# Longest products first in the scores, a shared reciprocal, an earlier column sum for the down factors, and two norms paced later

## The chip, the cores and the metric

The kernel runs on one core of one Trainium2 chip. The metric is the device time of one execution in microseconds (us); the time before is 2511.2 us, the median of three runs (2506.69 to 2511.34 us). Lower is better.

## What is computed

Two layers of a transformer over 1024 latent and 256 context tokens, width 1024, in float32. Cut to what matters here:

```python
for i in range(DEPTH):                                        # 2 layers
    h = modulate(rmsnorm(x, norm_pre_mix[i]), sh1, sc1)       # hc for the context tokens
    p = h @ w_in[i]                                           # queries, keys, values, Fourier channels
    attn = windowed_gqa_with_context(q, k, v, kc, vc, sink[i])
    four = fourier_mix(u, w_fourier[i])
    mix = concatenate([attn, four]) @ w_out[i]
    x_mid = x + g1 * rmsnorm(mix, norm_post_mix[i])
    hf = modulate(rmsnorm(x_mid, norm_pre_ffn[i]), sh2, sc2)
    x = x_mid + g2 * rmsnorm(swiglu(hf, w_gate[i], w_up[i], w_down[i]), norm_post_ffn[i])
# swiglu(h, g, u, d) = (silu(h @ g) * (h @ u)) @ d, hidden width 2816
# attention: 8 query heads, 2 key/value heads, head size 64; a query sees latent keys at
# distance <= 128, all 256 context keys and one sink logit per head, under one softmax
```

## The kernel before, in words

All activations stay in SBUF with channels on partitions (`X`: 128 x 8 x 1280). The tokens are worked on in two blocks, A and B: 640 tokens each in the first layer, 512 each in the second, where the context needs no output. Precision is built from pairs: each operand is split into a high and a low part, and a product is three matmuls (high x high, low x high, high x low). `gemm` (L518) does that for the input and output projections, `ffn_up` (L1084) for gate and up with seven half-size products in place of eight, `ffn_down` (L1215) for down, with its weights scaled and split on the way in (L1207 on ScalarE, L1208 on VectorE).

**Order.** The program is written as Python generators that `mix` interleaves: it always steps the one that is least far along for the cost that it was given, so `(side, 27)` means that the norm work beside a product is paced as if it had 27 steps. A bare `yield` in a generator is a step with nothing in it. The order in which the program emits instructions is their priority; the framework's scheduler (`schedule_with_timeline_sim=True`) then fixes the order on each engine's queue before the run, and `high_priority(offset=n)` moves what is inside it n places ahead. On the chip each queue runs in that order.

**Attention.** `Pair` handles two heads of one block of 128 queries. `score` (L191 to L216) fills a PSUM tile of two banks: the sink logit in one column (L197, a one-column product of a table of ones), the window of up to 384 latent keys (L201 high, L206 low, on the same bank), the two masks added as 128-column bf16 products with the identity (L203, L205), and 256 context keys (L207, L208). Then VectorE takes the negated row maximum (L215) and ScalarE the exponential with its sum `su` (L216). `turn` transposes the probabilities on TensorE (L226) and splits them (L230, L231). `value` multiplies by the values (L244); at its first step it makes a reciprocal tile of 128 columns out of the two sums of the two heads (L238), which `finish` transposes (L252) and multiplies in (L259). The attention runs beside the Fourier mixing and the projections of block B; there are 144 scores (16 of them for context queries, with no window) and 72 pairs.

**Norms.** `stats` squares and adds the eight tiles of a block, sums over partitions with one-column products (L667, tile `nps`) and computes the inverse root of the mean (L673 to L679, at high priority). `spread` (L689, tile `rps`) transposes that back over the tokens into a PSUM tile of the same pool (`sc`, two buffers) as the scores and the products of the projections, and copies it (L691). `postnorm` is `stats`, then `spread`, then eight steps: load the residual (SyncE's queue), scale (L712), add (L782 on VectorE or GpSimd), and store. `scaled` and `prenorm` do the norm ahead of a product.

**Layer turn.** Between the layers, the second block's `postnorm` runs beside the first three tiles of the next input projection (6, 7, 8); then the second block's `xstats` and `scaled` (the variable `side`) run beside tiles 1, 0, 2, 3, 4, 5 of it.

**Down factors.** After `ffn_up` each of the 11 chunks of the hidden layer has an exponent `he` per partition. `down_scale(blk)` makes of them and of the norms of the down weights a factor per chunk (`dn`) and one power of two for all partitions (`dback`). For the maximum over partitions it uses `highest` (L602 to L605): a product with the identity that lays the column out as a row, a VectorE maximum, and a product that spreads it back. `down_scale(0)` comes after the whole of `ffn_up`, `down_scale(1)` after the down product of block 0. Then `hidden` loads the spilled hidden chunks back from DRAM on SyncE's queue (L1189), and `ffn_down` loads the down weights on the same queue (L1202).

The steps of `ffn_up` are interleaved too: while the matrix `m` of `seq` takes its steps 1 to 5, the last two steps of the matrix before it are put between them. The last four matrices are (block 0, chunk 10, gate), (0, 10, up), (1, 10, gate), (1, 10, up).

Of the kernel before, what the change touches and what calls it, by code (L numbers as in the profile page):

```python
# [174 lines left out]
class Pair:  # L175
# [15 lines left out]
    def score(self, h):  # L191

        net, nc, w, g, n = self.net, self.nc, self.w, self.g, self.n
        s = net.sc.tile([P, 1024], F32, tag="sc", name="score")
        q = self.qs[:, 2 * self.u + h, :]
        hd = 4 * g + 2 * self.u + h
        nc.tensor.matmul(s[:, 511 - w:512 - w], net.bf1[:], net.sink[:, self.l, hd:hd + 1], start=True, stop=True)  # L197
        if w:
            loc = s[:, 512 - w:512]
            ls = slice(C + P * self.k0, C + P * self.k1)  # L200
            nc.tensor.matmul(loc, q, net.KHI[g][:, ls], start=True, stop=False)  # L201
            if n > 0:
                nc.tensor.matmul(loc[:, 0:P], net.bf[:, 0:P], net.bf[:, P:2 * P], start=False, stop=False)  # L203
            if n < NB - 1:
                nc.tensor.matmul(loc[:, w - P:w], net.bf[:, 0:P], net.bf[:, 2 * P:3 * P], start=False, stop=False)  # L205
            nc.tensor.matmul(loc, q, net.KLO[g][:, ls], start=False, stop=True)  # L206
        nc.tensor.matmul(s[:, 512:512 + C], q, net.KHI[g][:, 0:C], start=True, stop=False)  # L207
        nc.tensor.matmul(s[:, 512:512 + C], q, net.KLO[g][:, 0:C], start=False, stop=True)  # L208
        sv = s[:, 511 - w:512 + C]
        hs = slice(h, h + 1)  # L210
        p = net.PP[net.npp % len(net.PP)][:, 0:w + C + 1]
        net.npp += 1
        self.pp.append(p[:, 1:])
        with net.tc.high_priority(offset=AHEAD_OF):
            nc.vector.tensor_reduce(self.ng[:, hs], sv, axis=AX.X, op=ALU.max, negate=True)  # L215
            nc.scalar.activation(p, sv, AF.Exp, bias=self.ng[:, hs], accum_out=self.su[:, hs])  # L216
# [17 lines left out]
    def value(self, j):  # L234
        net, nc = self.net, self.nc
        if j == 0:
            self.out = net.qsp.tile([P, 2, P], F32, tag="pvl", name="pvl")
            nc.vector.reciprocal(self.out[:, 0].rearrange("p (h d) -> p h d", h=2), self.su[:].unsqueeze(2).broadcast_to([P, 2, HD]))  # L238
            self.pv = net.ps.tile([P, 384], F32, tag="ps", name="pv")
# [23 lines left out]
class Net:  # L263
# [504 lines left out]
    def postnorm(self, l, which, a, b, done=None, share=False, y=None):  # L768
# [5 lines left out]
        y = y or x  # L774
        yield from self.stats(y, w, "post")
        r = self.spread("post", w)
        for k in range(KD):
# [268 lines left out]
    def ffn_up(self, l, blocks, seq):  # L1046
# [92 lines left out]
        for m, after in zip(seq + [None], seq[1:] + [None, None]):  # L1139
# [4 lines left out]
            for n, who in enumerate((now, now, before, now, before, now, now)):  # L1144
                if who is not None and next(who, 0) is None:
                    yield c
                if n == 4 and after:
                    ready(after)
            before = now

# [13 lines left out]
    def down_scale(self, blk):  # L1164


        nc, r = self.nc, self.dn[blk]
        one = float(1 << 23)
        nc.vector.tensor_scalar(r[:].bitcast(I32), self.he[:, blk], one, -14 * one, op0=ALU.mult, op1=ALU.add)
        m = self.sm.tile([P, 2], F32, tag="fm", name="dm")  # L1170
        nc.vector.tensor_reduce(m[:, 0:1], r[:], axis=AX.X, op=ALU.max)
        nc.vector.scalar_tensor_tensor(m[:, 1:2], m[:, 0:1], m[:, 0:1], self.dmax[:], op0=ALU.mult, op1=ALU.mult)
        nc.vector.tensor_scalar(m[:, 1:2], m[:, 1:2], 1e-30, None, op0=ALU.max)
        self.power(self.dback[blk], self.highest(m[:, 1:2]).bitcast(I32), 24, 204)
        nc.vector.tensor_scalar(r[:], r[:], self.dback[blk][:, 0].bitcast(F32), None, op0=ALU.mult)

# [52 lines left out]
    def program(self):  # L1229
# [26 lines left out]
        for l in range(L):  # L1256
# [5 lines left out]
            else:  # L1262
                mix((self.inproj(l, 0, (6, 7, 8)), cost(3, KD, BW - C)), (first, 8))
                self.rope_tables()
# [3 lines left out]
            else:  # L1268
                mix((self.inproj(l, 0, (1, 0, 2, 3, 4, 5)), cost(6, KD, BW - C)), (side, 14))
            blocks = [A, B] if l == 0 else [(C, C + 512), (C + 512, T)]  # L1270
# [17 lines left out]
            def done(k, a, b, last=last):  # L1288
                if last:
                    nc.sync.dma_start(self.io["out"][:, k, a - C:b - C], self.X[:, k, a:b])  # L1290
                else:
# [4 lines left out]
                         self.prenorm(l, *blocks[0], "A", self.G[0]))  # L1296
            mix((self.outproj(l, *blocks[1]), cost(KD, KD, w)), (side, 27))
            self.G[1] = operands(l % 2)
# [7 lines left out]
            up = self.ffn_up(l, blocks, seq)  # L1306
            mix((part(up, 14 * AHEAD - 2), 2 * AHEAD * one), (side, 45))
            mix((part(up, 14 * AHEAD - 7), 2 * AHEAD * one), (self.down_norms(l), 24))
            mix((up, one * (44 - 4 * AHEAD)), (mod(0, 1), 64), (iter(()) if last else self.norms(l + 1), 2 * AHEAD))
            self.down_scale(0)  # L1310
            places = self.hidden(l, blocks)
# [4 lines left out]
            if not last:  # L1316
# [3 lines left out]
                side = chain(norm, self.xstats(*A, "A"), self.scaled(l + 1, 0, *A, "A"))  # L1320
                mix(down(1, 0, w, lambda m: self.X[:, m, a1:b1]), (side, 30), (pre, 8 * AHEAD))
                self.new_arena((l + 1) % 2)
# [41 lines left out]
```

## Time and profile before

| | before |
|---|---|
| runs | 2511.2, 2506.69, 2511.34 us |
| profiled execution: time | 2504.05 us |
| profiled execution: first to last instruction (span) | 2502.2 us |
| mean granted TensorE clock | 0.980 |
| TensorE matmul busy (PE) | 2352.4 us, 17224 instructions |
| VectorE busy (DVE) | 1787.2 us, 3462 instructions |
| ScalarE busy (ACT) | 1344.7 us, 2587 instructions |
| GpSimd busy (POOL) | 196.6 us, 204 instructions |
| DMA | 406.83 MB, mean 163 GB/s |

How to read it: the profile is of one execution, so a duration in it is set against 2504.05 us and not against the median. "Busy" for TensorE counts a matmul from its start to its modelled end, and matmuls overlap; the distance from one start to the next tells what one costs. "PEld" is the load of the stationary operand. A row of the timeline has the start and the length in us, the engine, the source line, the operation, what it writes and reads, and in brackets how long the engine stood idle before it and what ended that. A row of the windows has the busy time of each engine in a stretch, then the granted clock, the share of the DMA engines that was busy, and GB/s.

### The profile page before, as it was taken

To read this page: it belongs to the slowest core of one execution; us is meant where nothing else is said; L and a number is where in the kernel's file an instruction comes from. 1 tells how busy PE (TensorE), PEld (TensorE's weight loads), DVE (VectorE), ACT (ScalarE), POOL (GpSimd) and SP (SyncE) were. 2 spreads that over 40 slices of the span, in tenths; PEclk is the share of its full clock that TensorE was granted. 3 is DMA by queue.
4 is the path that set the end of the run, shared out by engine and by line. 5 is a ranking of instruction groups with operands and counts; after the bars stand their busy time and mean duration, and the time that the engine had idled before them with its cause. 6 is when DMAs were issued, how large, how long until landed. Compare 5 with 4: busy or idle time off the path is not lost. (4 is left out here: it accounts for less than half of the span.)

```text
span 2502.2 us, 44066 instructions
## 1 busy us (share of the span) xinstructions
PE 2352.4 (94%) x17224; PEld 1900.2 (76%) x17224; DVE 1787.2 (71%) x3462; ACT 1344.7 (54%) x2587; POOL 196.6 (8%) x204
## 2 busy tenths in 40 slices
PE   7998988999999999999999989989999999989997
PEld 5887877897776666666767779988778888874586
DVE  5588787767837887778774588797777577765485
ACT  4575556657525445434544345566674456545473
POOL 0222210010000000000000033210100000000000
PEclk9999989999999999999999989999999999999998
DMA  8535423568554344459873231101596422246474
GB/s 309 206 102 167 160 98 107 184 236 284 203 185 148 108 129 165 156 192 373 269 246 129 91 123 47 35 18 51 186 338 222 161 72 69 77 142 208 132 254 125
DMA packets 157377, 406.83 MB, mean 163 GB/s; under 512 B 17488, under 2 KB 34288, under 8 KB 157168
## 3 DMA queue, kind: packets, MB, share of 16 engines
q1 hardware_dynamic: 147952, 389.33, 46.2%
q10 hardware_dynamic: 9216, 14.68, 1.6%
q8 instruction: 135, 2.21, 0.4%
q14 instruction: 74, 0.61, 0.1%
HBM read 339.19 MB, written 64.76 MB: 161 GB/s over the span
## 5 line engine op out<-in xcount | busy, mean ns | idle before, releaser
L1084 PE MATMUL p<-ffn,ww 128*128 128x320 f16 (+1 forms) x7392 | 921.9, 287 | 25.5 <-ACT ww L464 5.5
L1084 PEld LDWEIGHTS <-ww 128*128 128x128 f16 x7392 | 722.7, 98 | 220.8 <-issue 23.5
L1215 PEld LDWEIGHTS <-wd 128*128 128x128 f16 x3696 | 363.6, 99 | 164.0 <-ACT wd L1207 5.8
L1215 PE MATMUL acc<-hid,wd 128*128 128x320 f16 (+2 forms) x2544 | 335.4, 294 | 3.5 <-ACT wd L1207 3.2
L1208 DVE SCALAR_TENSOR_TENSOR wd<-raw,dn,wd 128x256 f16<-128x256 f32 x440 | 186.4, 480 | 132.6 <-ACT wd L1207 132.0
L1207 ACT ACTIVATE wd<-raw,dn 128x256 f16<-128x256 f32 x440 | 187.2, 496 | 146.0 <-PE acc L1215 87.2
L518 PE MATMUL accn<-arena,hi 128*128 128x320 f32 (+1 forms) x992 | 252.2, 327 | 5.6 <-DVE X L259 2.0
L518 PE MATMUL acc<-arena,hi 128*128 128x320 f32 (+2 forms) x928 | 209.0, 330 | 5.6 <-ACT X L1038 3.8
L1215 PE MATMUL acc<-X,wd 128*128 128x320 f16 (+1 forms) x1152 | 195.0, 331 | 0.9 <-ACT wd L1207 0.9
L518 PEld LDWEIGHTS accn<-arena,hi 128*128 128x128 f32 x992 | 173.2, 190 | 16.3 <-DVE arena L231 2.7
L518 PEld LDWEIGHTS acc<-arena,hi 128*128 128x128 f32 x928 | 154.8, 190 | 23.4 <-ACT X L1038 5.3
L518 PE MATMUL accn<-arena,lo 128*128 128x320 f32 (+1 forms) x496 | 159.8, 325 | 1.7 <-DVE lo L400 1.7
L674 POOL TENSOR_TENSOR nr<-nm,mhalf 128x5 f32<-128x5 f32 (+2 forms) x17 | 18.2, 1069 | 1708.0 <-DVE nm L673 1708.0
L465 DVE SCALAR_TENSOR_TENSOR ww<-raw,sp,ww 128x1024 f16<-128x1024 f32 x112 | 125.4, 1147 | 27.3 <-ACT ww L464 27.1
L464 ACT ACTIVATE ww<-raw,sp 128x1024 f16<-128x1024 f32 x112 | 109.9, 1033 | 59.4 <-DVE raw L479 51.0
L400 DVE TENSOR_TENSOR lo<-raw,hi 128x1024 fp32r<-128x1024 f32 x77 | 101.6, 1320 | 55.0 <-ACT hi L399 39.9
L230 ACT CAST arena<-tp 128x512 fp32r<-128x512 f32 (+1 forms) x184 | 96.6, 528 | 76.6 <-PE tp L226 74.2
L216 ACT ACTIVATE A<-score,ng 128x641 f32<-128x641 f32 (+2 forms) x144 | 106.6, 741 | 46.9 <-PE tp L226 30.1
L215 DVE TENSOR_REDUCE ng<-score 128x1 f32<-128x641 f32 (+2 forms) x144 | 106.3, 740 | 28.6 <-PE score L208 27.3
L518 PE MATMUL acc<-arena,lo 128*128 128x320 f32 (+2 forms) x464 | 125.0, 327 | 0.1
L399 ACT CAST hi<-raw 128x1024 fp32r<-128x1024 f32 x77 | 80.6, 1047 | 75.1 <-PE acc L518 28.7
L448 ACT ACTIVATE junk<-raw 128x1024 bf16<-128x1024 f32 x88 | 92.3, 1051 | 42.1 <-DMA raw<-in_wup 19.2
(231 smaller groups left out, 3724.4 us busy)
## 6 DMA issues: line engine op xcount, KB each, us to landing
raw<-in_wdown SPq DMA_DIRECT2D x112, 512.0 KB, 4.6
ww<-wc SPq DMA_DIRECT2D x96, 512.0 KB, 4.3
raw<-in_wgate SPq DMA_DIRECT2D x60, 512.0 KB, 4.6
raw<-in_wup SPq DMA_DIRECT2D x60, 512.0 KB, 4.4
wm<-in_wada SPq DMA_DIRECT2D x96, 256.0 KB, 4.3
raw<-in_wdown SPq DMA_DIRECT2D x56, 384.0 KB, 4.2
raw<-in_win SPq DMA_DIRECT2D x40, 512.0 KB, 3.6
wada<-in_wada SPq DMA_DIRECT2D x39, 512.0 KB, 4.4
```

The costliest lines, as they stand in the source:

```text
L215: nc.vector.tensor_reduce(self.ng[:, hs], sv, axis=AX.X, op=ALU.max, negate=True)
L216: nc.scalar.activation(p, sv, AF.Exp, bias=self.ng[:, hs], accum_out=self.su[:, hs])
L230: nc.scalar.copy(ph, tp[:, 0:256 * n])
L400: nc.vector.tensor_tensor(lo[:, 0:w], raw[:, 0:w], hi[:, 0:w].bitcast(F32), op=ALU.subtract)
L448: self.nc.scalar.activation(junk[:], raw[j][:], AF.Square, accum_out=self.ss[:, j, i:i + 1])
L464: nc.scalar.activation(hi, src, AF.Copy, scale=s)
L465: nc.vector.scalar_tensor_tensor(lo, src, s, hi, op0=ALU.mult, op1=ALU.subtract)
L518: self.nc.tensor.matmul(ps, wt[:, ks], xt[:, a:b], start=(k == 0 and i == 0), stop=(k == n - 1 and i == 2))
L1084: nc.tensor.matmul(ps, w[:, at:at + P], G[:, k, x, c, 0:h], start=(start and k + t == 0), stop=(k == KD // 2 - 1 and t == 2), skip_group_c ...
L1207: nc.scalar.activation(wt[:, 0, c], raw[:, c], AF.Copy, scale=r)
L1208: nc.vector.scalar_tensor_tensor(wt[:, 1, c], raw[:, c], r, wt[:, 0, c], op0=ALU.mult, op1=ALU.subtract)
L1215: nc.tensor.matmul(out, wt[:, e, k], xs[x][:, s, u:v], start=(f + s + i == 0), stop=(f == NP - 1 and s == 1 and i == 2))
```

## The change

- `score`: the order of its products on TensorE. Before: sink, high window, masks, low window, context. After: high window, low window, context high and low, then the masks, then the sink.
- `value`: the reciprocal is taken of the two columns in place, and a copy spreads it over the 128 columns.
- `postnorm`: two empty steps between `stats` and `spread`. The costs given to `mix` for the norms go up where they hold a postnorm (8 to 9, 27 to 29, 45 to 46, 30 to 32). For the second block's norm ahead of the next layer's input projection the cost goes from 14 to 10, so its steps come later relative to the product.
- `down_scale`: in place of the maximum over partitions a sum over partitions, as one product of a bf16 table of ones with a 16-bit column; all at high priority. `down_scale(0)` is emitted within `ffn_up`, after the second step of the last matrix.

```diff
@@ score
-        nc.tensor.matmul(s[:, 511 - w:512 - w], net.bf1[:], net.sink[:, self.l, hd:hd + 1], start=True, stop=True)
         if w:
             loc = s[:, 512 - w:512]
             ls = slice(C + P * self.k0, C + P * self.k1)
             nc.tensor.matmul(loc, q, net.KHI[g][:, ls], start=True, stop=False)
-            if n > 0:
-                nc.tensor.matmul(loc[:, 0:P], net.bf[:, 0:P], net.bf[:, P:2 * P], start=False, stop=False)
-            if n < NB - 1:
-                nc.tensor.matmul(loc[:, w - P:w], net.bf[:, 0:P], net.bf[:, 2 * P:3 * P], start=False, stop=False)
-            nc.tensor.matmul(loc, q, net.KLO[g][:, ls], start=False, stop=True)
+            nc.tensor.matmul(loc, q, net.KLO[g][:, ls], start=False, stop=False)
         nc.tensor.matmul(s[:, 512:512 + C], q, net.KHI[g][:, 0:C], start=True, stop=False)
         nc.tensor.matmul(s[:, 512:512 + C], q, net.KLO[g][:, 0:C], start=False, stop=True)
+        if w:
+            if n > 0:
+                nc.tensor.matmul(loc[:, 0:P], net.bf[:, 0:P], net.bf[:, P:2 * P], start=False, stop=(n == NB - 1))
+            if n < NB - 1:
+                nc.tensor.matmul(loc[:, w - P:w], net.bf[:, 0:P], net.bf[:, 2 * P:3 * P], start=False, stop=True)
+        nc.tensor.matmul(s[:, 511 - w:512 - w], net.bf1[:], net.sink[:, self.l, hd:hd + 1], start=True, stop=True)
@@ value
-            nc.vector.reciprocal(self.out[:, 0].rearrange("p (h d) -> p h d", h=2), self.su[:].unsqueeze(2).broadcast_to([P, 2, HD]))
+            nc.vector.reciprocal(self.su[:], self.su[:])
+            nc.vector.tensor_copy(self.out[:, 0].rearrange("p (h d) -> p h d", h=2), self.su[:].unsqueeze(2).broadcast_to([P, 2, HD]))
@@ postnorm
         yield from self.stats(y, w, "post")
+        yield
+        yield
         r = self.spread("post", w)
@@ ffn_up
                 if n == 4 and after:
                     ready(after)
+                if n == 1 and m == (1, NP - 1, 1):
+                    self.down_scale(0)
@@ down_scale
-        nc.vector.tensor_scalar(m[:, 1:2], m[:, 1:2], 1e-30, None, op0=ALU.max)
-        self.power(self.dback[blk], self.highest(m[:, 1:2]).bitcast(I32), 24, 204)
+        with self.tc.high_priority(offset=1000):
...
+            nc.vector.tensor_scalar(sq[:], m[:, 1:2], 1e-30, None, op0=ALU.max)
+            ps = self.ps.tile([P, 8], F32, tag="ps", name="dsum")[:, 0:1]
+            nc.tensor.matmul(ps, self.bf1[:], sq[:], start=True, stop=True)
+            self.power(self.dback[blk], ps.bitcast(I32), 24, 204)
@@ program
-                mix((self.inproj(l, 0, (6, 7, 8)), cost(3, KD, BW - C)), (first, 8))
+                mix((self.inproj(l, 0, (6, 7, 8)), cost(3, KD, BW - C)), (first, 9))
-                mix((self.inproj(l, 0, (1, 0, 2, 3, 4, 5)), cost(6, KD, BW - C)), (side, 14))
+                mix((self.inproj(l, 0, (1, 0, 2, 3, 4, 5)), cost(6, KD, BW - C)), (side, 10))
-            mix((self.outproj(l, *blocks[1]), cost(KD, KD, w)), (side, 27))
+            mix((self.outproj(l, *blocks[1]), cost(KD, KD, w)), (side, 29))
-            mix((part(up, 14 * AHEAD - 2), 2 * AHEAD * one), (side, 45))
+            mix((part(up, 14 * AHEAD - 2), 2 * AHEAD * one), (side, 46))
-            self.down_scale(0)
-                mix(down(1, 0, w, lambda m: self.X[:, m, a1:b1]), (side, 30), (pre, 8 * AHEAD))
+                mix(down(1, 0, w, lambda m: self.X[:, m, a1:b1]), (side, 32), (pre, 8 * AHEAD))
```

More of the change, by code (lines that the diff above doesn't have):

```diff
@@ L1168, in down_scale @@
         one = float(1 << 23)
[L1169 to L1173, printed above, removed]
-        self.power(self.dback[blk], self.highest(m[:, 1:2]).bitcast(I32), 24, 204)
-        nc.vector.tensor_scalar(r[:], r[:], self.dback[blk][:, 0].bitcast(F32), None, op0=ALU.mult)
+        with self.tc.high_priority(offset=1000):
+            nc.vector.tensor_scalar(r[:].bitcast(I32), self.he[:, blk], one, -14 * one, op0=ALU.mult, op1=ALU.add)
+            m = self.sm.tile([P, 2], F32, tag="fm", name="dm")
+            sq = self.sm.tile([P, 1], BF16, tag="sq", name="dq")
+            nc.vector.tensor_reduce(m[:, 0:1], r[:], axis=AX.X, op=ALU.max)
+            nc.vector.scalar_tensor_tensor(m[:, 1:2], m[:, 0:1], m[:, 0:1], self.dmax[:], op0=ALU.mult, op1=ALU.mult)
+            nc.vector.tensor_scalar(sq[:], m[:, 1:2], 1e-30, None, op0=ALU.max)
+            ps = self.ps.tile([P, 8], F32, tag="ps", name="dsum")[:, 0:1]
+            nc.tensor.matmul(ps, self.bf1[:], sq[:], start=True, stop=True)
+            self.power(self.dback[blk], ps.bitcast(I32), 24, 204)
+            nc.vector.tensor_scalar(r[:], r[:], self.dback[blk][:, 0].bitcast(F32), None, op0=ALU.mult)
     def hidden(self, l, blocks):
```

## The prediction

> **What bounds the kernel now.** I read the page first, then TensorE's busy time in the two stretches of attention, then TensorE's own waits, and then a timeline at each place that the edits touch.
>
> ```profile
> PE 2352.4 (94%) x17224; PEld 1900.2 (76%) x17224; DVE 1787.2 (71%) x3462; ACT 1344.7 (54%) x2587; POOL 196.6 (8%) x204
> ```
> ```profile
> 99.00:500.00 401.00, 361.18 (x2519) 319.14 (x2518) 314.90 (x565) 252.85 (x538) 61.79 (x72) 0.97 0.44 145
> 1509.00:1766.00 257.00, 246.11 (x1756) 225.19 (x1755) 203.73 (x386) 156.69 (x359) 50.77 (x60) 0.99 0.12 37
> ```
> ```profile
> PE score L197 <- ACT A L216: 15.1, 15, 2.3
> PE rps L689 <- DVE nr L679: 14.4, 7, 6.5
> PE fps L605 <- DVE hm L1121: 6.5, 2, 3.5
> ```
>
> TensorE is busy 94% of the span, so only two things shorten the run: cheaper matmul sequences, and TensorE's waits. The first two columns of the windows are the length of the stretch and TensorE's busy time: it idles 401.0 - 361.2 = 39.8 us in attention of layer 1 and 10.9 us in layer 2. VectorE (fourth number) is at 79% in both. Three of the largest rows of TensorE's waits are places that the change touches: the score buffer, the transposes of a norm, the factors of down.
>
> **Scores.** One two-mask score, and full-clock products of 384 columns behind each other:
>
> ```profile
> 254.27 0.17 PE L197 MATMUL score<-sink,bf 128*128 128x1 bf16 x1
> 254.30 0.42 PE L201 MATMUL score<-arena,qs 128*128 128x384 f32 x1
> 254.56 0.23 PE L203 MATMUL score<-bf 128*128 128x128 bf16 x1
> 254.62 0.22 PE L205 MATMUL score<-bf 128*128 128x128 bf16 x1
> 254.65 0.42 PE L206 MATMUL score<-arena,qs 128*128 128x384 f32 x1
> 254.91 0.28 PE L207 MATMUL score<-arena,qs 128*128 128x256 f32 x1
> 255.03 0.28 PE L208 MATMUL score<-arena,qs 128*128 128x256 f32 x1
> 255.15 0.18 PE L197 MATMUL score<-sink,bf 128*128 128x1 bf16 x1
> ```
> ```profile
> 1422.54 0.52 PE L518 MATMUL acc<-arena,hi 128*128 128x384 f32 x2
> 1422.90 0.33 PE L518 MATMUL acc<-arena,lo 128*128 128x384 f32 x1
> ```
>
> From start to start a score costs 255.15 - 254.27 = 0.88 us. Two products of 384 take 0.36 where they follow each other, 0.18 each; here each takes 0.26, because the short product ahead of it doesn't cover its weight load (0.08 us is left over). In the new order both 384s cost 0.18, the 256s stay at 0.12, the masks at 0.06 and the sink at 0.03, and one uncovered load of 0.08 remains, for whatever follows the sink: 0.36 + 0.24 + 0.12 + 0.03 + 0.08 = 0.83. That is 0.05 us on 128 scores with a window, **-6.4 us**. The 16 context scores keep their products, and swap the uncovered load only. Ends: 0, if what follows the sink loses both loads, and 0.08 x 128 = -10, if what follows covers its own. VectorE waits for the last product as before, so the maximum isn't later.
>
> **Reciprocal.**
>
> ```profile
> L238 DVE RECIPROCAL pvl<-su 128x128 f32<-128x128 f32 x72 | 68.3, 948 | 4.6 <-ACT A L216 3.4
> L259 DVE TENSOR_TENSOR X<-pvl,pv 128x128 f32<-128x128 f32 x72 | 20.5, 284 | 2.1
> L1121 DVE TENSOR_SCALAR hm<-hm 128x1 f32<-128x1 f32 x44 | 6.5, 149 | 0.5
> ```
>
> No row has a two-column reciprocal or a 128-column copy. The smallest VectorE operation takes 149 ns, one over 128 columns 284. I take 149 + 284 = 433 ns in place of 948: 515 ns x 72 = 37 us less of VectorE (ends 2 x 149 and 2 x 284: 47 and 27). VectorE isn't the bound, so this counts only where TensorE waits for something queued behind VectorE. The score waits (15.1 us) end with the exponential, which waits for a maximum on that queue. Of the 50.7 us of idle time in the two stretches I take one eighth, **-6 us**; ends 0 (each wait has another work as its cause) and -15 (those score waits).
> The Trainium skill (VectorE: DVE Perf Modes, section on the TRN2 errata) speaks against splitting: every instruction pays a fixed latency, 58 cycles plus one per element at 0.96 GHz. My estimate from its table for the pair is 63 + 194 = 257 ns, which would make 50 us of VectorE time out of 37. The row of 149 ns for one column says that the fixed part is larger here, and the row decides.
>
> **Down factors.** Layer 1, then layer 2:
>
> ```profile
> 1108.97 0.15 DVE L1173 TENSOR_SCALAR dm<-dm 128x1 f32<-128x1 f32 x1
> ```
> ```profile
> 1111.67 1.80 PE L1084 MATMUL p<-ffn,ww 128*128 128x320 f16 x12
> 1117.02 0.38 PE L605 MATMUL fps<-hx,cst 1*128 1x1 f32 x2 [3.54 <-DVE hm L1121]
> 1121.14 9.09 PE L1215 MATMUL acc<-X,wd 128*128 128x320 f16 x50
> 1139.44 6.58 PE L1215 MATMUL acc<-hid,wd 128*128 128x320 f16 x36 [3.24 <-ACT wd L1207]
> ```
> ```profile
> 1121.00:1126.00 5.00, 5.00 (x22) 2.97 (x23) 5.00 (x13) 2.65 (x6) 0.00 (x0) 0.55 1.04 400
> ```
> ```profile
> 1138.88 2.95 ACT L1207 ACTIVATE wd<-raw,dn 128x256 f16<-128x256 f32 x7 [7.86 <-DMA raw<-in_wdown]
> ```
> ```profile
> 2241.43 2.79 PE L1084 MATMUL p<-ffn,ww 128*128 128x256 f16 x24
> 2247.23 0.38 PE L605 MATMUL fps<-hx,cst 1*128 1x1 f32 x2 [3.01 <-DVE hm L1121]
> 2250.87 12.49 PE L1215 MATMUL acc<-X,wd 128*128 128x512 f16 x47
> ...
> 2267.09 8.15 PE L1215 MATMUL acc<-X,wd 128*128 128x512 f16 x37
> ```
> ```profile
> 2263.11 2.11 ACT L1207 ACTIVATE wd<-raw,dn 128x256 f16<-128x256 f32 x5 [8.32 <-DMA raw<-in_wdown]
> ```
>
> In layer 1 the last product of up ends at 1113.47 and down runs freely from 1121.14: 7.7 us, in which TensorE does two products. The cause is order on VectorE: the column is ready at 1109.1, but the maximum of the row waits behind the last block's work. Then the clock is at 0.55 for 5 us, another 2.2 us lost; together 9.9. In layer 2 it is 2250.87 - 2244.22 = 6.7 and, at the same clock, about 2.2: 8.9. The new chain from the column is one product (0.4), three VectorE steps of `power` and one for `dn` (four times about 0.15), one ScalarE scaling (0.5): ready near 1111, ahead of 1113.47.
> But layer 1 has a second lock: the DMA engines are full (share 1.04, 400 GB/s), and ScalarE gets the third block of down weights only at 1138.9, behind the reloads of the hidden chunks on SyncE's queue. If that landing doesn't move, what down gains at 1113 it loses at 1139. It moves only as far as the earlier scaling frees the weight buffer and the scheduler puts the load earlier. Ends 0 and -9.9; I take **-4**. In layer 2 ScalarE has 15 chunks scaled before it waits for the next load until 2263.1; they feed 15 x 6 products of 512 columns, at 8.15 / 37 = 0.22 us 19.8 us of work. An early start at 2244.7 uses them up by 2264.5: just enough. **-7** (ends -4 and -8.9). What is left to fear is the wait that the change adds: `dsum` stands in TensorE's queue within the last products, which wait behind it if VectorE is late with the column, and ScalarE and VectorE for them; up to 3.5 us a layer (today's wait), which the ends take in. VectorE's eight short steps of about 0.15, 1.2 us, now stand ahead of the last block's evacuation; the seven products after the second step of the last matrix cover them. `down_scale` issues no DMA, so SyncE's queue keeps its order but for buffers that come free earlier.
>
> **Layer turn.**
>
> ```profile
> 1451.22 0.46 PE L518 MATMUL acc<-arena,hi 128*128 128x320 f32 x2
> 1453.93 0.77 PE L830 MATMUL vps<-cst,vt 128*128 128x128 f32 x5 [2.26 <-ACT vt L825]
> 1456.85 2.29 PE L667 MATMUL nps<-cst,ssq 128*128 128x1 f32 x10 [2.15 <-DVE ssq L661]
> 1465.67 1.30 PE L689 MATMUL rps<-cst,nr 128*128 128x128 f32 x5 [6.53 <-DVE nr L679]
> 1466.62 0.67 PE L518 MATMUL acc<-arena,hi 128*128 128x384 f32 x1
> ```
> ```profile
> 1467.00:1472.00 5.00, 5.00 (x21) 5.00 (x21) 4.27 (x6) 0.69 (x1) 0.00 (x0) 0.67 0.00 0
> ```
>
> Tile 2 of the projection starts at 1466.6 only because the transposes stand ahead of it and take one of the two `sc` buffers. With 10 in place of 14 they stand at 7/10 of the planned work and not at 7/14, behind most of tile 2, so 6.5 us of wait can go, and the slow clock after it (0.67 for 5 us: 1.7). Against it: the postnorm ahead (spread at 7/9, not 5/8, of 3 x 24 products x 0.18 = 13 us) starts its scaling 2.0 us later, its residual loads and stores on SyncE's queue too, so the sums (`nps`) may hold TensorE 2 us longer. **-7**; ends 0 and -14, all waits from 1451.7 to 1466.6 and the clock.
> The Trainium skill (TensorE: Matmul & The Clock Gate, Part 1) says that the clock halves after an idle window of about 3.4 us. By it the waits of 2.3 and 2.2 us, if they stay two, would leave the clock whole, and with 2 us more in one piece it would fall again, for 1.7 us. The rows here can't tell which of the three waits brought it down.
>
> **Norms elsewhere.**
>
> ```profile
> 1300.01 1.30 PE L689 MATMUL rps<-cst,nr 128*128 128x128 f32 x5 [2.58 <-DVE nr L679]
> 529.53 0.73 PE L689 MATMUL rps<-cst,nr 128*128 128x128 f32 x5 [0.47 <-DVE nr L679]
> 586.86 4.75 PE L1084 MATMUL p<-ffn,ww 128*128 128x320 f16 x24 [2.90 <-ACT A L1088]
> ```
>
> The two empty steps let 2.6 + 0.5 us of wait pass, with slowed transposes some 4. On the other side each postnorm beside the output projection starts its scaling 7/29 - 5/27 of a product about as long as the 57 us between the last two rows, 3.2 us, later, and the FFN start hangs on that chain (586.9). I take +0.75 each: **-2.5**, ends -6 and +4.
>
> **Sum.** 6.4 + 6 + 4 + 7 + 7 + 2.5 = 33 us off 2504.05, so 2471 for such an execution. It is 7 us under the median of 2511.2, so for a median 2478.
>
> **Rivals.** (1) *The waits move on.* Layer 1's down start stays locked by the weight landing, and the turn by its sums. Only scores, layer 2's start with -4, and norms stay: -13, 2498. For it: the full DMA engines at 1121. Against: the third load's buffer does come free earlier. (2) *VectorE was the hidden bound of attention.* -15 there in place of -6, and -14 at the turn: -49, with the upper end of layer 1's start -55, 2456. For: 79% busy; against: TensorE's waits there end on many engines. (3) *Slower.* The later scaling becomes what TensorE waits for: 2.0 us from the postnorm, 4.6 us from 7/10 in place of 7/14 of the 23 us that `cost` gives the six tiles, and 3.2 us at each FFN start, 13 us, with nothing gained at the turn or at down, against 9 from scores and norms: +4, 2515. It decides once block B's operands are later than the attention and tile 9 that run ahead of them. Against: TensorE's waits show no row for these operands now. (4) *No change in order.* The scheduler leaves `rps` and `dsum` where they stood, and the VectorE time is off the path: near 0 but for the scores, 2507.
>
> **Numbers.** Forecast 0.52 (own range 2461 to 2493), rival 1 0.25, rival 2 0.12, rival 3 0.08, rival 4 0.03. A measurement tells 0.2%, 5 us, from no change. Faster: 0.52 + 0.20 of rival 1 + 0.12 + 0.01 = 0.85; same 0.08 (the rest of rivals 1 and 4, a little of 3); slower 0.07. Range 2458 to 2502: it cuts half of rival 2, rival 3 and the ends of 1 and 4.
>
> **What would show it.** Right: a two-mask score at 0.83 us; reciprocal and copy under 0.5 us together; no VectorE maximum of a row between up and down, and down starting within 2 us of up in layer 2; `rps` at the turn without a wait and no granted clock near 0.67 behind it. Wrong: the wait for down weights in layer 1 grown from 7.9 us by what the start gained (rival 1), or new TensorE waits at the FFN starts or ahead of block B's projection (rival 3).

## The result, and the profile after

The changed kernel takes **2486.57 us** in the median (2485.83 to 2493.53) beside 2509.36 us of the kernel before: a ratio of 0.9917, 95% interval 0.9903 to 0.9932, so 17 to 24 us less. The forecast was 2478, with 2458 to 2502 as its range. The sign came out, the down factors are the largest part, as forecast, and the size is 9 us off. Two of the terms have the wrong sign (the reciprocal and the turn), and that of the down factors is larger than predicted, so part of the agreement is luck.

The profiled execution of after is the longest of its four (2493.53 us, span 2491.3, clock 0.977; the others 0.980), and the one of before is shorter than its median. A comparison of the two pages shows 11 us of the 23. Busy times of after, then TensorE in the two stretches of attention (that of layer 2 begins and ends 5 us later than in before's rows), then its own waits:

```profile
PE 2344.3 (94%) x17212; PEld 1905.1 (76%) x17212; DVE 1750.7 (70%) x3530; ACT 1344.1 (54%) x2587; POOL 201.2 (8%) x204
```
```profile
99.00:500.00 401.00, 361.24 (x2539) 323.29 (x2537) 297.19 (x605) 255.46 (x541) 67.44 (x72) 0.95 0.44 149
1514.00:1771.00 257.00, 246.03 (x1786) 230.17 (x1787) 190.35 (x425) 160.46 (x367) 50.05 (x60) 0.99 0.13 43
```
```profile
PE score L200 <- ACT A L217: 11.0, 10, 2.3
PE acc L1226 <- ACT wd L1218: 9.0, 2, 8.6
PE rps L691 <- DVE nr L681: 8.9, 5, 3.8
```

VectorE lost 36.5 us of work, and TensorE idles 39.8 and 11.0 us in the two stretches, as it did before (39.8 and 10.9). The waits for down's factors are gone from the list; in their place stands one for a weight of down, 8.6 us long.

A score (start of its first product to the start of the next score's), and the two operations in place of the reciprocal of 948 ns:

```profile
251.42 0.42 PE L200 MATMUL score<-arena,qs 128*128 128x384 f32 x1
251.68 0.34 PE L201 MATMUL score<-arena,qs 128*128 128x384 f32 x1
251.85 0.28 PE L202 MATMUL score<-arena,qs 128*128 128x256 f32 x1
...
252.21 0.17 PE L209 MATMUL score<-sink,bf 128*128 128x1 bf16 x1
252.24 0.42 PE L200 MATMUL score<-arena,qs 128*128 128x384 f32 x1
```
```profile
L240 DVE COPY pvl<-su 128x128 f32<-128x128 f32 x72 | 17.7, 246 | 1.1
L239 DVE RECIPROCAL su<-su 128x2 f32<-128x2 f32 x72 | 11.5, 160 | 8.4 <-ACT A L217 7.7
```

0.82 us in place of 0.88; 406 ns in place of 948. The start of down in layer 1 on TensorE, ScalarE's wait for the weight, and the windows around it (the last three columns are the granted clock, the DMA engines' share and GB/s); then layer 2:

```profile
1120.00 0.17 PE L1184 MATMUL dsum<-dq,bf 128*128 128x1 bf16 x1
1120.03 1.79 PE L1088 MATMUL p<-ffn,ww 128*128 128x320 f16 x12
1122.17 0.45 PE L1226 MATMUL acc<-X,wd 128*128 128x320 f16 x2 [0.35 <-ACT wd L1218]
...
1144.39 5.90 PE L1226 MATMUL acc<-hid,wd 128*128 128x320 f16 x26 [8.65 <-ACT wd L1218]
```
```profile
1143.83 2.96 ACT L1218 ACTIVATE wd<-raw,dn 128x256 f16<-128x256 f32 x7 [9.88 <-DMA raw<-in_wdown]
```
```profile
1122.00:1132.00 10.00, 9.65 (x70) 6.77 (x71) 10.00 (x21) 5.18 (x11) 0.00 (x0) 1.00 1.03 390
1132.00:1144.00 12.00, 3.74 (x29) 2.55 (x27) 4.19 (x12) 2.06 (x3) 0.00 (x0) 0.78 1.04 403
1144.00:1160.00 16.00, 15.61 (x99) 10.43 (x100) 12.76 (x28) 8.60 (x16) 0.00 (x0) 0.85 1.04 410
```
```profile
2239.05 0.17 PE L1184 MATMUL dsum<-dq,bf 128*128 128x1 bf16 x1
2239.08 2.78 PE L1088 MATMUL p<-ffn,ww 128*128 128x256 f16 x24
2241.70 4.48 PE L1226 MATMUL acc<-X,wd 128*128 128x512 f16 x20
...
2266.79 4.05 PE L1226 MATMUL acc<-hid,wd 128*128 128x512 f16 x18
```

Both starts are as meant: `dsum` waits for nothing, and down begins 0.65 and 0.11 us after the last start of a product of up (6.08 and 5.30 before). In layer 2 nothing comes behind. In layer 1 TensorE then stands still for 8.65 us where before stood for 3.24: the start gained 5.4 and the wait is 5.4 longer, with the DMA engines full from 1122 to 1160 us.

The turn to layer 2, with the last sum of squares on VectorE that `nps` waits for:

```profile
1456.86 1.33 PE L834 MATMUL vps<-cst,vt 128*128 128x128 f32 x5 [3.83 <-ACT vt L829]
...
1468.99 1.64 PE L669 MATMUL nps<-cst,ssq 128*128 128x1 f32 x10 [4.38 <-DVE ssq L663]
1474.45 1.30 PE L691 MATMUL rps<-cst,nr 128*128 128x128 f32 x5 [3.82 <-DVE nr L681]
```
```profile
1467.33 1.61 DVE L663 TENSOR_TENSOR ssq<-ssq,sq 128x640 f32<-128x640 f32 x1
```

Tile 2 runs ahead of the sums, as planned, but the three waits are 12.0 us in place of 10.9, and from down's last product to the first score it is 70.79 us in place of 67.14.

### The profile page after: what moved, and what is told of

It reads as the page before. It is cut to its first block, busy times and chain, and to the rows that moved or that the text cites. A ratio compares the mean times of both kernels' runs of the same rounds, so it can differ in the third digit from the quotient of the medians.

```text
span 2491.3 us, 44186 instructions
## 1 busy us (share of the span) xinstructions
PE 2344.3 (94%) x17212; PEld 1905.1 (76%) x17212; DVE 1750.7 (70%) x3530; ACT 1344.1 (54%) x2587; POOL 201.2 (8%) x204
## 5 line engine op out<-in xcount | busy, mean ns | idle before, releaser
L450 ACT ACTIVATE junk<-raw 128x1024 bf16<-128x1024 f32 x88 | 92.4, 1051 | 50.7 <-DMA raw<-in_wup 20.5
```

What stands on the lines that cost most here:

```text
L450: self.nc.scalar.activation(junk[:], raw[j][:], AF.Square, accum_out=self.ss[:, j, i:i + 1])
```

## The experiments

T1 is the sum of the prediction, T2 its rival "the waits move on". Every kernel was timed beside the kernel before:

| kernel | median us | ratio to before, 95% | that in us |
|---|---|---|---|
| after, the whole change | 2486.57 | 0.9917 (0.9903 to 0.9932) | -21 (-24 to -17) |
| e1 scores alone | 2501.51 | 0.9970 (0.9959 to 0.9980) | -7.5 (-10 to -5) |
| e2 reciprocal alone | 2524.32 | 1.0056 (1.0040 to 1.0072) | +14 (+10 to +18) |
| e3 down factors alone | 2490.98 | 0.9927 (0.9911 to 0.9943) | -18 (-22 to -14) |
| e4 pacing alone | 2507.31 | 0.9993 (0.9981 to 1.0004) | -2 (-5 to +1) |
| e7 reciprocal in layer 2 alone | 2504.86 | 0.9991 (0.9981 to 1.0002) | -2 (-5 to +0.5) |
| e12 reciprocal in one place | 2508.01 | 0.9998 (0.9986 to 1.0010) | -0.5 (-3.5 to +2.5) |
| e6 after, reciprocal undone | 2480.66 | 0.9898 (0.9884 to 0.9913) | -26 (-29 to -22) |
| e8 after, turn undone | 2482.65 | 0.9900 (0.9886 to 0.9915) | -25 (-29 to -21) |
| e10 after, both undone | 2481.83 | 0.9897 (0.9884 to 0.9911) | -26 (-29 to -22) |
| e5 after, reload later | 2489.28 | 0.9925 (0.9912 to 0.9938) | -19 (-22 to -16) |
| e9 after, weight ahead of reload | 2489.44 | 0.9928 (0.9916 to 0.9941) | -18 (-21 to -15) |
| e11 e10 and e9 | 2484.33 | 0.9898 (0.9883 to 0.9912) | -26 (-29 to -22) |

The intervals are 3 to 4 us to a side, so the parts were also read by stages in all fourteen traces: the length of a stage from the start of its first product to that of its last, and in it TensorE's idle time, which is the sum of its gaps of over 0.1 us. Kernels whose program is the same up to a stage show what one execution is worth there: attention of layer 1 took 406.8 to 411.7 us in five of them, up of layer 1 536.7 to 540.2 in four.

**e1, scores alone.** The hunk `score` of the change, on the kernel before:

```diff
-            nc.tensor.matmul(loc, q, net.KLO[g][:, ls], start=False, stop=True)
+            nc.tensor.matmul(loc, q, net.KLO[g][:, ls], start=False, stop=False)
...
+        nc.tensor.matmul(s[:, 511 - w:512 - w], net.bf1[:], net.sink[:, self.l, hd:hd + 1], start=True, stop=True)
```

> The kernel before with the first edit alone: in a score the long products first, then the masks, the sink last. Theory T1 (the sum of the prediction): 128 scores of 0.05 us less each, 6.4 us off the two attentions (0 to 10), about 2503 us against 2509.4, nothing in the FFN. Theory T2 (waits move on): the score itself goes from 0.88 to 0.83 us, but attention shrinks by less than that, because the score's next wait for its bank takes part of it back: 2 to 4 us. Both expect a score with two masks of 0.83 us; if it stays at 0.88, both have the edit's effect wrong.

-7.5, as T1 has it; T2's 2 to 4 is below the interval. The gain lies in layer 2: attention takes 277.0 us in the mean of the four kernels with this edit and the old reciprocal (275.5 to 278.5), 283.3 in the four with neither (283.0 to 283.5). In layer 1 it is 408.0 against 409.4, inside the spread. T1 has 3.2 us a layer; of layer 2's 6.3 some belong to the clock, since two of the four (275.5 and 275.7) lack the half-clock stretch of 6.83 us that the other two (278.4 and 278.5) and before have. This run also shows a wait that is not of the edit, TensorE's and VectorE's rows in down(1) of layer 1:

```profile
1305.08 1.30 PE L690 MATMUL rps<-cst,nr 128*128 128x128 f32 x5 [8.32 <-DVE nr L680]
```
```profile
1295.47 1.28 DVE L1209 SCALAR_TENSOR_TENSOR wd<-raw,dn,wd 128x256 f16<-128x256 f32 x3 [4.39 <-ACT wd L1208]
1298.85 1.68 DVE L1209 SCALAR_TENSOR_TENSOR wd<-raw,dn,wd 128x256 f16<-128x256 f32 x4 [2.10 <-ACT wd L1208]
1301.12 1.68 DVE L1209 SCALAR_TENSOR_TENSOR wd<-raw,dn,wd 128x256 f16<-128x256 f32 x4 [0.59 <-ACT wd L1208]
1302.72 0.16 DVE L674 TENSOR_SCALAR nm<-nps 128x5 f32<-128x5 f32 x1
```

`nps` had been asked for at 1290.3, but the small step `nm` stands behind eleven splits of weights, which wait for a weight from DRAM. The same wait is 2.58 us in before, 2.67 in e7 and 4.04 in e12, whose programs are the same up to there: its length hangs on when weights land.

**e2, e7, e12, the reciprocal: everywhere, in layer 2, in one place.** The `value` hunk on the kernel before; in e7 under the first condition, in e12 under the second:

```diff
+            if self.l == 0:                                                      # e7
+            if not (self.l == 1 and (self.n, self.g, self.u) == (0, 0, 0)):      # e12
                 nc.vector.reciprocal(out, su)
+            else:
+                nc.vector.reciprocal(self.su[:], self.su[:])
+                nc.vector.tensor_copy(out, su)
```

> The kernel before with the second edit alone: the reciprocal of two columns and a broadcast copy in place of one reciprocal of 128 columns. Both theories expect about 37 us less busy time of VectorE. T1: an eighth of TensorE's 50.7 us of idle time in attention goes with it, -6 us (0 to -15). T2: the waits in attention are for ScalarE's spreading of the exponentials (the score's banks) and not for VectorE, so TensorE gains 0 to 3 us. The rival in which VectorE is the hidden bound expects -15 us or more from this edit alone.

> The kernel before with the pair of column reciprocal and copy in layer 2's attention alone; up to there every instruction stands as in before. Theory A (order): layer 2's attention falls by 4 to 5 us (283.5 before, 278.8 with the edit in both layers), layer 1 stays as it was, and what comes behind layer 2's attention may move by some us either way: 2501 to 2508 in all. Theory B (the instruction itself): about half of the edit's loss shows, +5 to +8, with layer 2's attention the longer one.

> The kernel before with the pair of column reciprocal and copy in one single place of the 72 (first query of layer 2's attention): half a microsecond of VectorE's work at most. The planner's order of VectorE and ScalarE in the FFN of layer 2 is another one behind it. Order theory (an edit's cost is in the order that the planner writes for what comes behind, not in its own work): the FFN of layer 2 moves by some us (417.0 us up's length before; 427 with the pair in all of layer 2's attention), 2506 to 2516 in all. Work theory: nothing moves, within 1.5 us of before's median.

Alone the edit makes the kernel 14 us slower, which neither theory expected, nor the rival in which VectorE is the hidden bound. By stages against before: attention of layer 1 +4.9, up +4.9, down +5.2 (of which 3.9 is the wait for `rps` just described, 6.47 us here), attention of layer 2 -4.6, up of layer 2 +6.2. So its work is a gain where it can be seen by itself (layer 2: 278.84 and 278.86 us in e2 and e7, idle time 9.8 in both against 12.2), and the losses lie mostly in stages in which it has no instruction. The +4.9 in attention of layer 1 is in no other kernel with the edit (407.4 to 409.5 us in after, e5, e8 and e9). e7 shows the same in one layer: -4.6 in attention, then +10.0 in up behind it, 427.05 us against 417.04 (3.5 us more idle time and 10.2 us more at half clock).

What the edit brings into up is another order. Read by source line, tile and shape, TensorE's, VectorE's and ScalarE's instructions of up of layer 2 stand in e2 and e7 in one order that none of the other twelve traces has, and these two are the longest (423.28 and 427.05 us). Seven kernels have before's order, and take 417.0 to 418.9 us: after, e5 and e8, which hold the edit in all 72 places, are among them, and so is e12. e12's order in up is thus before's, other than its expectation says, and its 418.25 us leave the question open that it was made for. Other traces answer it: e1, e9 and e11 have other orders again and take 417.7 to 418.8 us, and e6 and e10 share one more and take 421.18 us each. So the loss in up goes with the order and not with the edit's work, and another order need not cost; which of its swaps costs up 6 to 10 us is not shown.

**e3, down factors alone.**

```diff
+                if n == 1 and m == (1, NP - 1, 1):
+                    self.down_scale(0)
...
-            self.down_scale(0)
...
-        self.power(self.dback[blk], self.highest(m[:, 1:2]).bitcast(I32), 24, 204)
+            nc.tensor.matmul(ps, self.bf1[:], sq[:], start=True, stop=True)
+            self.power(self.dback[blk], ps.bitcast(I32), 24, 204)
```

> The kernel before with the third edit alone: the factors of down(0) by one 16-bit sum, asked for within the last product of up, and those of down(1) by the same sum. T1: the start of down comes 5.4 us earlier in layer 1 and 5.2 us earlier in layer 2, and keeps -4 and -7, -11 in all (down(1) of layer 2 gains 2 to 3 of it). T2: in layer 1 the start moves but the first wait for a weight of down, behind the reloading of hidden, grows by what the start gained (about 8 to 9 us where before's has 7.9 after a start 5.4 later), so layer 1 keeps 0 to 2 and layer 2 its 7: -7 to -9 in all.

-18, the largest part by far, and above what either theory gave it. Layer 1 does what T2 says: a free start, then a wait of 8.67 us. From the end of up to the end of down it takes 301.93 us in place of 308.88 (after: 301.93 too). Layer 2 takes 231.49 in place of 240.25. In layer 1 e3 also has no wait for `rps`, though its norm is paced as before. TensorE's and VectorE's rows of e3 there:

```profile
1292.92 1.17 PE L667 MATMUL nps<-cst,ssq 128*128 128x1 f32 x10
1296.84 0.16 DVE L673 TENSOR_SCALAR nm<-nps 128x5 f32<-128x5 f32 x1
```

`nm` runs 3.9 us behind `nps`, in before 6.7: the splits ahead of it had begun before `nps` was asked for. So a part of e3's gain is this wait, and e4 takes away the same one.

**e4 and e8, the pacing alone, and the turn undone in after.**

```diff
 e4 (on before)
+        yield
+        yield
...
+                mix((self.inproj(l, 0, (1, 0, 2, 3, 4, 5)), cost(6, KD, BW - C)), (side, 10))
 e8 (on after)
-                mix((self.inproj(l, 0, (6, 7, 8)), cost(3, KD, BW - C)), (first, 9))
+                mix((self.inproj(l, 0, (6, 7, 8)), cost(3, KD, BW - C)), (first, 8))
-                mix((self.inproj(l, 0, (1, 0, 2, 3, 4, 5)), cost(6, KD, BW - C)), (side, 10))
+                mix((self.inproj(l, 0, (1, 0, 2, 3, 4, 5)), cost(6, KD, BW - C)), (side, 14))
...
+        if not turn:
             yield
             yield
```

> The kernel before with the fourth edit alone: two empty steps in every postnorm and the five changed costs of the side work (9, 10, 29, 46, 32). T1: -7 at the turn to layer 2 and -2.5 elsewhere, -9.5 in all. T2: the turn's three waits (2.26, 2.15 and 6.53 us before) become three others of 12 us in sum, +1 to +4 there with a half-clock window the more, and elsewhere -3 to -4 (the two waits at 529 and 1300 us), so -3 to +1 in all.

> The kernel after with the turn to layer 2 as before: no empty steps in the postnorm of down's second block there, and the costs 8 and 14 again; the other four costs and the empty steps of the other norms stay. Theory T1 of the prediction (the pacing is a gain at the turn, 7 us): undone it costs 4 to 7 us, 2491 to 2494. Theory T2 (the sums are only asked for later and the same chain ends 4 us later): undone it gives 2 to 4 us back, 2483 to 2485, with waits of 2.3, 2.2 and 6.5 us at the turn in place of 3.8, 4.4 and 3.8.

T2 is right on the turn. The rows of e8, where the waits are before's again:

```profile
1447.02 1.04 PE L835 MATMUL vps<-cst,vt 128*128 128x128 f32 x5 [2.28 <-ACT vt L830]
1449.94 2.29 PE L669 MATMUL nps<-cst,ssq 128*128 128x1 f32 x10 [1.88 <-DVE ssq L663]
1458.82 1.30 PE L691 MATMUL rps<-cst,nr 128*128 128x128 f32 x5 [6.58 <-DVE nr L681]
```

Over all traces the turn takes 66.3 to 67.9 us with the old pacing (nine kernels, mean 67.4) and 68.9 to 70.8 with the new one (five, mean 69.8). The two groups don't touch: +2.4 us. Elsewhere the pacing by itself is a gain: in e4 the wait for `rps` is gone and down of layer 1 takes 305.37 us in place of 308.88, and in none of the kernels with the empty steps has `rps` a wait there. Undoing the turn takes 4 us off after's median, near the edge of what the intervals tell.

**e5, e9, e11, the weight that down waits for in layer 1.** On SP the third block of wdown stands behind 26 of the 28 loads of hidden in after's trace (the expectations say 28). In e5 the second block's loads are spread over down(0) (17 ahead of it), in e9 tied behind that weight's issue (6 ahead); e11 is e9 on e10.

```diff
-        for blk in range(2):
-            for f in range(KEPT if blk == 0 else 0, NP):
...
+        def behind():
+            yield 4
+            with self.tc.issue_after(self.lead.ins):
+                loads(1)
+        loads(0)
...
-                mix(down(0, 0, w, first), (part(pre, 4 * AHEAD), 4 * AHEAD), (side, 32))
+                mix(down(0, 0, w, first), (part(pre, 4 * AHEAD), 4 * AHEAD), (side, 32), (later, 32))
```

> The kernel after, with one thing moved: the loads that bring hidden's second block back are emitted beside the tiles of down(0) and not all ahead of it, so that the third block of wdown stands behind 17 of these loads on SP and no longer behind 28. Theory A: the 8.65 us for which TensorE waits at 1144.39 us of after's profile, and the half-clock window behind it (10.2 us, so 5 lost), are the queue of loads. 11 loads fewer ahead, of 320 KB at about 400 GB/s, bring that weight 9 us earlier; the wait goes, and the time falls by 8 to 13 us against after, to about 2476. Theory B: the wait is for something else (the splitting of the weight by ScalarE and VectorE, or DMA bandwidth that is full anyway), and stays within 2 us of what it is: no change against after (2486.6).

> The kernel after, with the reload of hidden's second block in layer 1 tied on SP behind the issue of the third block of wdown: that one now stands behind the 6 loads that down(0) itself needs, where it stood behind 28 in after and behind 17 in the experiment before, which took only 2.1 us off the wait of 8.65 us, since its own landing took 12 us behind the loads in flight. Theory A (the loads ahead in the DMA queues are the wait): 6 loads of 320 KB at about 400 GB/s are 5 us from the first issue, the block lands before it is wanted, the wait goes and with it the half-clock window behind it (10.2 us, 5 lost): 8 to 13 us less than after, 2474 to 2479. Theory B (the wait is for DMA bandwidth that is full whatever comes first): the wait moves to a later block of wdown or to down(1)'s start, and the time stays within 3 us of after's 2486.6.

> The last two together: after without the reciprocal's edit, with the turn as before and the third block of wdown ahead of the reload of hidden's second block in layer 1. By Theory A of the reload 8 to 13 us below the kernel without that move, about 2466. By Theory B the same as it, about 2477.

Theory B's number: no gain in any of the three. TensorE in e5, then TensorE, ScalarE and the windows in e9:

```profile
1128.78 6.85 PE L1228 MATMUL acc<-hid,wd 128*128 128x320 f16 x36 [6.54 <-ACT wd L1220]
1137.68 2.63 PE L1228 MATMUL acc<-X,wd 128*128 128x320 f16 x13 [2.05 <-ACT wd L1220]
```
```profile
1149.07 3.38 PE L1236 MATMUL acc<-X,wd 128*128 128x320 f16 x12 [8.89 <-ACT wd L1228]
```
```profile
1148.51 1.70 ACT L1228 ACTIVATE wd<-raw,dn 128x256 f16<-128x256 f32 x4 [6.35 <-DMA raw<-in_wdown]
```
```profile
1125.00:1135.00 10.00, 9.88 (x73) 6.66 (x72) 6.46 (x16) 4.90 (x10) 0.00 (x0) 1.00 1.04 406
1135.00:1150.00 15.00, 6.11 (x43) 3.95 (x41) 4.43 (x10) 3.45 (x7) 0.00 (x0) 0.83 1.04 410
```

In e5 the wait splits into 6.54 and 2.05; in e9 the third block is there in time and the fifth is late, by 8.89. The sum stays at 8.6 to 8.9. Theory B's reason, DMA engines that are full whatever comes first, isn't shown by this. In e9 SP still issues 13 of the reloads between the fourth block and the fifth:

```profile
1124.11 0.33 SPq L1221 DMA_DIRECT2D raw<-in_wdown  x1
1124.89 4.04 SPq L1200 DMA_DIRECT2D hid<-hs  x5
...
1135.40 5.85 SPq L1200 DMA_DIRECT2D hid<-hs  x8
1141.79 0.33 SPq L1221 DMA_DIRECT2D raw<-in_wdown  x1
```

And the engines are full (a share of 1.03 to 1.04, 390 to 410 GB/s) for a time only. In after's trace they have room ahead of down's start and from 1200 us on:

```profile
1110.00:1120.00 10.00, 10.00 (x76) 7.16 (x74) 6.38 (x14) 2.27 (x4) 0.00 (x0) 1.00 0.54 177
1200.00:1300.00 100.00, 100.00 (x740) 72.37 (x739) 74.99 (x140) 60.16 (x111) 0.00 (x0) 1.00 0.79 274
```

Shown is that one weight put ahead of the reloads moves the wait to a weight that still stands behind them. An order that holds the reloads of the second block back until the engines have room wasn't tried, so whether the order alone can take the 8.6 us away stays open.

**e6 and e10, the reciprocal undone in after, and both undone.** e6 puts back the old line of `value`, e10 that and e8's edit:

```diff
-            nc.vector.reciprocal(self.su[:], self.su[:])
-            nc.vector.tensor_copy(self.out[:, 0].rearrange("p (h d) -> p h d", h=2), self.su[:].unsqueeze(2).broadcast_to([P, 2, HD]))
+            nc.vector.reciprocal(self.out[:, 0].rearrange("p (h d) -> p h d", h=2), self.su[:].unsqueeze(2).broadcast_to([P, 2, HD]))
```

> The kernel after with the reciprocal of before (one instruction of 128 columns): the other three edits stay. Alone the edit made the kernel 15 us slower. Theory A (its work is a gain or at nothing, the loss alone was an unlucky order written by the planner for that kernel): undone here it costs 0 to 6 us, so 2486 to 2493. Theory B (the edit itself is a loss, through its extra instruction in VectorE's queue): undone here it gives 10 to 15 us back, about 2473.

> The kernel after without the edit of the reciprocal and with the turn as before: scores, down factors and the pacing of the other norms are what is left of the change. If what each undoing gave adds up (5.9 us and 3.9 us), 2476 to 2478. If the two gains are one (the planner's order of the turn), 2480 to 2483. In the account of the prediction, in which both edits were gains (6 and 7 us), 2499.

Without the reciprocal's edit the change is 6 us better by the medians, without the turn's 4, without both 5: the gains don't add, and each interval overlaps after's. That neither edit gives the 6 or 7 us forecast for it is beyond the intervals; by how much they hurt is not. The three kernels, and e11 with them, agree at 0.9897 to 0.9900 and are the best of all.

## Why the prediction was right or wrong

**Scores: right.** 0.82 us a score for 0.83, -7.5 us for -6.4. The uncovered weight load was the mechanism: where the two products of 384 follow each other, the second starts 0.17 us before its successor (251.68 to 251.85) and no longer 0.26.

**Reciprocal: the failed step is "of the 50.7 us of idle time in the two stretches I take one eighth".** The price of the operations was good (406 ns for 433) and VectorE's busy time fell by 36.5 us for 37, but TensorE's idle time stayed at 50.7. By itself in layer 2 the edit does take 2.4 us of idle time; beside the shorter scores it takes none (12.1 to 12.7 us in the four kernels with both edits, 11.6 to 11.8 in the four with scores alone, 12.2 to 12.5 with neither). The share of one eighth had no row behind it; why nothing of the 2.4 us is left beside the shorter scores, no run shows. By the prediction's estimate from the Trainium skill's table (VectorE: DVE Perf Modes, the TRN2 errata) the pair would take 257 ns; the rows say 406, and the row of 149 ns was the better guide. Below its table the Trainium skill says in the same section that this row is too low and that the fixed part was measured at about 150 cycles, by my estimate 156 ns at its 0.96 GHz. The 160 ns of the two-column reciprocal agree with that.

**Down factors: the size of layer 2, and more.** Layer 2 gave 8.2 us in after and 8.8 in e3 for the 7 taken, within the ends. Layer 1 looks like rival 1 (start -5.4, wait +5.4), but the landing moved too. SyncE's issue of the weight that TensorE waits for, before and after:

```profile
1134.33 0.80 SPq L1202 DMA_DIRECT2D raw<-in_wdown  x2
1137.85 1.16 SPq L1213 DMA_DIRECT2D raw<-in_wdown  x2
```

The last product of up starts at 1113.18 us in before and at 1121.52 in after. The load is issued 21.2 and 16.3 us behind it, and the wait ends 26.3 and 22.9 us behind it. These 3.4 us are what the term had as -4. The clock gave back little there: the later wait brings a stretch at half clock of its own (0.78 and 0.85 in the windows), and up to 1165 us both kernels have 10.2 us of it. The stage is 7.0 us shorter in all; the other 3.5 are the wait for `rps`, which e4 takes away without the new factors. In e3 the two stages together are 15.7 us shorter; the rest of its 18 +- 4 can't be told from the spread.

**Turn: the failed step is "the sums (`nps`) may hold TensorE 2 us longer".** In before the last sum of squares ends 34.7 us after down's last product, in after 45.5 (1467.33 + 1.61 - 1423.44): 10.8 later, not 2. Tile 2 was moved ahead of it and fills 6.8 of these microseconds; the rest made the waits of 2.26 and 2.15 into 3.83 and 4.38. The term priced the first step that moved, and that one too low (the scaling L714 starts 16.0 us after down's last product in place of 11.8, 4.2 later), and not the chain behind it. So of the 6.53 us for `rps`, which were to go, 3.82 are left, and the other two waits took the gain.

On the clock there, two windows of before:

```profile
1449.00:1456.60 7.60, 3.44 (x24) 2.94 (x22) 7.18 (x10) 5.51 (x9) 0.00 (x0) 1.00 0.75 228
1456.60:1463.40 6.80, 2.29 (x10) 2.20 (x10) 5.08 (x12) 2.72 (x4) 3.12 (x3) 0.50 0.22 78
```

It is whole up to 1456.60 and half from there on, at the end of the second short wait and ahead of the long one. The Trainium skill's rule (TensorE: Matmul & The Clock Gate, Part 1: half clock after an idle window of about 3.4 us) would have left it whole, with one wait of 2.26 and one of 2.15. Here two short waits close together were enough (in the 3.41 us up to 1456.60 TensorE worked for 0.77), and the measurement decides.

**Norms elsewhere: right, for one of its reasons.** In down of layer 1 `rps` has no wait left in after; the start of the FFN of layer 1 waits as it did:

```profile
1310.62 0.71 PE L691 MATMUL rps<-cst,nr 128*128 128x128 f32 x5
591.31 1.96 PE L1088 MATMUL p<-ffn,ww 128*128 128x320 f16 x11 [2.90 <-ACT A L1092]
```

With the empty steps TensorE has work for 14.1 us from `nps` to `rps` there, with the old pacing for 6.5. The wait was 2.6 to 8.3 us long in five of the six traces with the old pacing, and missing in e3. The one at 533 us stays 0.47 long. Nothing is seen of the +0.75 or of rival 3.

**The sum.** Scores -7.5 and down -18 make -25.5. e10, which has both and the pacing of the other norms, measures -26: the pacing adds nothing there, since e3 loses the same wait for `rps` (3.5 us in e4) without it. The turn adds +2.4, which leaves some 2 us of loss for the reciprocal up to the -21 of the whole; the intervals don't tell these from 0 or from the 5 that e6 puts on it. Against the forecast of -33, the terms of 6, 7 and 2.5 became losses of some 2 and 2 and nothing, so 20 us of forecast gain are missing; down gave 7 more and scores 1 more. That 2478 came within 9 us of the result is luck to this extent: misses of both signs stand in the sum.

## What to carry to other kernels

Work taken off an engine that isn't the bound has the price of the waits that end on it, each by its row, and edits that take away the same wait share one such price (here the one for `rps`: 3.5 us, and not twice). Where the DMA engines are full, an earlier start of the consumer is in part given back at the first transfer that is late. Putting one transfer ahead moved the wait to the next one here. Where a planner writes the order, compare the order of the traces before blaming an edit's own work, and time each edit by itself and undone in the whole: here parts of -7.5, +14, -18 and -2 made -21, and the profile of one execution did not tell a change of 5 us from the spread.

## What the runs showed of the hardware that was not expected

- The half-clock stretches in the clock records of these traces are, but for the one at the end of the run, 3.41, 6.83, 10.24, 13.65 or 17.07 us long, multiples of 3.41, and they last beyond the wait that brings them on. What goes ahead of one is a stretch in which TensorE works little. Cut into stretches of 3.41 us on the grid of the records, the fourteen traces have 140 at the whole clock in which TensorE is busy for less than 40%, and a half-clock one follows every one of them. Of the 9072 that are busy for 75% or more, none is followed by one; in between both occur. So short waits add up, and it counts where a wait falls: one of 2.26 us halves the clock from 1459.62 us on in e1, and one of 2.32 us, up to 197.52 us, leaves it whole in before.
- The same program, up to a place, has a wait of 2.6, 2.7 or 4.0 us at that place (before, e7 and e12: `rps` in down of layer 1; and of 8.3 in e1, where only scores far ahead of it differ), since one step of 0.16 us on VectorE stands behind operations that wait for a DMA.
- A reciprocal of two columns takes 160 ns and one of 128 columns 948: 6.3 ns for each further column, where the copy of 128 columns takes 246 in all.
